# Another order of the matmuls inside a unit: how the walks over the eight rows turn, where the next unit goes on, and where z and b units begin

## Chip, core and metric

The kernel runs on one core of a Trainium2 chip. The metric is the device time of one execution in microseconds (us); the median of several runs counts. TensorE (PE, with its weight loads PEld), VectorE (DVE), ScalarE (ACT), GpSimd (POOL) and SyncE (SP, which here only issues DMAs) run beside each other.

## What is computed

One inference step of a hybrid decoder layer over 336 tokens: 16 meta and 256 prompt tokens, and 8 sequences of 8 new tokens. The parts that matter here, cut from the reference:

```python
h = rms_norm(x, norm_w)
proj = h @ w_in                     # 2048 -> 22592 columns
z, xbc, dt_raw, sc_b, sc_c, sc_h, sc_z, g_a, g_b = split_proj(proj)
xbc = silu(causal_dwconv(xbc, conv_prev, ssd_conv_w) + ssd_conv_b)
...                                 # Mamba-2 SSD over xs, B, C, dt -> y
y_a = gated_group_rms_norm(y, z, ssd_norm_w) @ w_ssd_out
u_c = causal_dwconv(sc_c * sc_h, sconv_prev, sconv_w)
y_b = (sc_b * u_c * silu(sc_z)) @ w_sconv_out
merged = sigmoid(g_a) * y_a + sigmoid(g_b) * y_b
out = x + merged @ w_o
```

All of it is float32. Almost all of the time is the matrix products, above all `h @ w_in`.

## The kernel before, in words

Activations lie with the channel on the partition: `hx` (L73) holds, for each of 16 row tiles k of 128 channels, the 336 tokens of `h`, once as a rounded high part (`hhi`) and once as the rest (`hlo`). One row tile is 336 floats, 1344 bytes of a partition. A **unit** (L128) makes 128 output columns for all tokens. It has two halves; each half takes 512 KB of weights (`wblk`, L96): a DMA to `wraw`, a copy on ACT to `whi`, a difference on DVE to `wlo`. These two hold eight blocks of 128 columns, 144 floats (576 bytes) apart, and the whole block is shifted by 16 floats (64 bytes) times `at` (L93).

A half then has 24 matmuls into one PSUM tile `pj` (`mm`, L123): for each of the eight rows k the three products hi·xh, hi·xl and lo·xh. So a unit has 48 matmuls, each with its own weight load. Which row comes when is set by the **plan** (`terms`, L116), and only by that; the sum is the same. `RISE` goes through rows 0 to 7 three times. `LAST` begins with row 7. `FALL2` goes down by two rows: 6 4 2 0 for hi·xh and hi·xl, then a turn by +7 to 7 5 3 1 for hi·xl, hi·xh and lo·xh, then a turn by +5 to 6 4 2 0 for lo·xh.

Units come one after another on PE, with two PSUM tiles in turn:

- Start: tiles 0 to 2 of the short convolution, partly before the norm is known (`uproj`, from `uhi` and `ulo`).
- Tiles j = 3 to 15 of the short convolution (L323), four units each: **c** (`FALL2`, 324 tokens, `at` 0) and **h** (`RISE`, 324 tokens, `at` = j mod 4) in `conv_in` (L236), then **z** and **b** (`RISE`, 320 tokens, `at` 0).
- 16 pairs of a gate unit and a unit of `w_sconv_out` (`LAST`), with the tables of the scan between them.
- Eight groups g of the scan. Each has six convolution units (`conv_tile`, L469): B and four x tiles with 336 tokens (`FALL2`, `at` 1), C with 324 tokens (`FALL2`, `at` 2), and four z units (`z_units`, L508, `RISE`, 320 tokens), with the scan's own steps, output units and some gates woven between them (L787).
- The rest: output units, gates, and the projection with `w_o`.

The queues of the other engines have the work of a unit in the order in which it is written. Nothing else orders the matmuls.

Of the kernel before, what the change touches and what calls it, by code (L numbers as in the profile page):

```python
# [9 lines left out]
AF = mybir.ActivationFunctionType  # L10
# [39 lines left out]
def tile_hybrid_step(ctx, tc, xT, w0, w1, w2, wdt, wso, wsc, wo, cmask, vec, hvec, convst, sconvst, xe_, fwe, h0T,  # L50
                     yA, yB, yE, convo, ssmp, ssms, sconvo):
    nc = tc.nc
# [37 lines left out]
    latest = {}  # L90
    AT_V, AT_Y, AT_O, AT_X, AT_C, AT_SC = 1, 3, 3, 1, 2, 0

# [20 lines left out]

    RISE, LAST, FALL2 = range(3)

    def terms(plan, hi, lo, xh, xl, nk):  # L116
        if plan == FALL2:
            even, odd = (list(range(i, nk, 2))[::-1] for i in range(2))
            return [(w, x, k) for w, x, q in ((hi, xh, even), (hi, xl, even), (hi, xl, odd), (hi, xh, odd), (lo, xh, odd),
                                              (lo, xh, even)) for k in q]  # L120
        return [(w, x, (k - (plan == LAST)) % nk) for w, x in ((hi, xh), (hi, xl), (lo, xh)) for k in range(nk)]

    def mm(out, hi, lo, xh, xl, base, nk, k0, first, last, plan=RISE):  # L123
        for i, (w, x, k) in enumerate(terms(plan, hi, lo, xh, xl, nk)):
# [3 lines left out]
    def unit(src, xh, xl, n, plan=RISE, at=0):  # L128
        pt = ps.tile([P, 512], F32, name="pj")
        for half in range(2):  # L130
            hi, lo = wblk(src[:, half * 1024:half * 1024 + 1024], at)
            mm(pt[:, :n], hi, lo, xh, xl, 0, 8, half * 8, half == 0, half == 1, plan)
        return pt[:, :n]

    def proj(src, t0, plan=RISE, at=0):
        return unit(src, lambda k: hhi[:, k, t0:T], lambda k: hlo[:, k, t0:T], T - t0, plan, at)
# [44 lines left out]
    with tc.tile_pool(name="pa", bufs=2) as pa:  # L181
# [50 lines left out]

        def uproj(src, t0, plan=RISE, at=0):
            return unit(src, lambda k: uhi[:, k, t0:T], lambda k: ulo[:, k, t0:T], T - t0, plan, at)

        def conv_in(j, pr, pre=None, fac=None, between=None):  # L236
            c_s = pa.tile([P, T - TC], F32, name="c_s")
            if fac is None:
                nc.scalar.activation(c_s, pre[0] if pre else pr(w2[16 + j], TC, FALL2, AT_SC), AF.Copy)
            else:  # L240
                nc.vector.tensor_tensor(c_s, pr(w2[16 + j], TC, FALL2, AT_SC), fac, mult)
            if between:
                between()
            ph = pre[1] if pre else pr(w2[32 + j], TC, at=j % 4)
            up = pa.tile([P, 338], F32, name=f"up{j}" if j < 2 else "up", bufs=1 if j < 2 else 2)
            ups = eights(up[:, 258:338], 10)
            nc.vector.tensor_tensor(up[:, :258], c_s[:, 2:260], ph[:, 2:260], mult)  # L247
            nc.vector.tensor_tensor(ups[:, :, 2:10], eights(c_s[:, 260:]), eights(ph[:, 260:]), mult)
            return up, ups
# [209 lines left out]
    with tc.tile_pool(name="pb", bufs=2) as pb:  # L459
# [588 lines left out]
```

## Time and profile before

| | |
|---|---|
| median of 3 runs | 1791.15 us (1789.12 to 1791.41) |
| the profiled execution | 1786.97 us |
| its span, first to last instruction | 1785.2 us |
| PE busy | 1776.8 us, 13006 matmuls |
| DVE, ACT, POOL busy | 1147.4, 829.1, 392.7 us |
| DMA | 331.33 MB, 186 GB/s over the span |
| granted clock of TensorE over the span | 0.999 |

The profiled execution took 1.8 us more than its span, and 4.2 us less than the median of the runs. A matmul is recorded for about 300 ns, but the next begins after some 140 ns; so its busy time says little, and the distance from start to start is the number to read. The timeline merges equal matmuls into one row: start, duration until the last of them ends, operands, and their count. The start of the next row less the start of this one, over the count, is the pace of PE.

### The profile page before, as it was taken

The numbers are of one execution on the slowest core, as the hardware profiler recorded it, in microseconds if no ns is written. First come the engines' busy times: TensorE is split into PE (matmuls) and PEld (weight loads), VectorE is DVE, ScalarE is ACT, GpSimd is POOL, SyncE is SP. The second block draws the span as 40 slices with busy tenths as digits, with TensorE's granted clock in tenths as the row PEclk, the third lists the DMA queues.
The fourth block names the chain that finished last, engine by engine and source line by source line (L and its number), as shares of the span: only waits on it lengthen the run. The fifth ranks groups of instructions, "written<-read, shape, count | busy, mean of one in ns | idle before, by whom it ended". The sixth has DMA issues, their size and how long they took to land.

```text
span 1785.2 us, 32410 instructions
## 1 busy us (share of the span) xinstructions
PE 1776.8 (100%) x13006; PEld 1760.2 (99%) x13006; DVE 1147.4 (64%) x1696; ACT 829.1 (46%) x1269; POOL 392.7 (22%) x398
## 2 busy tenths in 40 slices
PE   9999999999999999999999999999999999999998
PEld 9999999999999999999999999999999999999998
DVE  7845544454543335658587787877878778776644
ACT  6433333333333334646656354564546546443543
POOL 0100000000000001243262432534334253400012
PEclk9999999999999999999999999999999999999999
DMA  7444444444454557457567574665756657577553
GB/s 258 150 150 147 153 153 151 146 152 150 156 167 160 167 167 234 154 177 240 172 207 231 175 249 158 210 221 184 246 159 213 216 175 253 159 245 220 188 182 130
DMA packets 117286, 331.33 MB, mean 186 GB/s; under 512 B 20944, under 2 KB 37904, under 8 KB 117136
## 3 DMA queue, kind: packets, MB, share of 16 engines
q1 hardware_dynamic: 116272, 327.89, 56.2%
q8 instruction: 102, 1.67, 0.4%
q10 hardware_dynamic: 864, 1.38, 0.2%
q14 instruction: 48, 0.39, 0.1%
HBM read 296.34 MB, written 32.88 MB: 184 GB/s over the span
## 4 chain that ended last, share of the span: by engine, by line
PE 90%; DVE 4%; DMA 3%; ACT 2%; issue 1%; POOLq 0%; SPq 0%; POOL 0%; ACTq 0%; DVEq 0%
PE pj L125 83%; DMA wraw<-w 2%; PE yb L662 2%; DVE wlo L102 1%; DMA ssms<-h 1%; PE ms L648 1%; PE pj L230 1%; DVE h L728 1%; DVE cacc L483 1%; ACT whi L101 1%; PE yb L597 1%; ACT W L571 1%; PE pj L874 1%; PE ms L230 0%; PE ms L546 0%
## 5 line engine op out<-in xcount | busy, mean ns | idle before, releaser
L125 PE MATMUL pj<-hx,whi 128*128 128x320 f32 (+2 forms) x5760 | 899.9, 308 | 0.0
L125 PEld LDWEIGHTS pj<-hx,whi 128*128 128x128 f32 x5760 | 851.6, 188 | 4.6 <-ACT pad L474 1.7
L102 DVE TENSOR_TENSOR wlo<-wraw,whi 128x1024 fp32r<-128x1024 f32 x470 | 599.5, 1276 | 389.2 <-PE pj L125 193.2
L101 ACT ACTIVATE whi<-wraw 128x1024 fp32r<-128x1024 f32 x470 | 496.6, 1058 | 727.6 <-PE pj L125 592.0
L125 PE MATMUL pj<-hx,wlo 128*128 128x320 f32 (+2 forms) x2880 | 476.3, 307 | 0.0
L125 PEld LDWEIGHTS pj<-hx,wlo 128*128 128x128 f32 x2880 | 433.2, 188 | 0.0
L608 POOL TENSOR_TENSOR h<-h,decS 128x512 f32<-128x512 f32 x64 | 76.4, 1228 | 141.8 <-PE ms L648 141.8
L253 POOL COPY SCS<-up 128x2 f32<-128x2 f32 x16 | 20.9, 1307 | 353.1 <-DVE up L247 322.9
L125 PE MATMUL pj<-yh,whi 128*128 128x320 f32 x512 | 95.0, 307 | 1.5 <-ACT zs L515 0.8
L125 PE MATMUL pj<-yl,whi 128*128 128x320 f32 x512 | 93.5, 304 | 0.0
L125 PE MATMUL pj<-yh,wlo 128*128 128x320 f32 x512 | 93.4, 304 | 0.0
L483 DVE SCALAR_TENSOR_TENSOR cacc<-pad,V,cacc 128x360 f32<-128x360 f32 (+1 forms) x144 | 90.2, 626 | 2.0
L756 DVE TENSOR_TENSOR yan<-yan,pj 128x320 f32<-128x320 f32 x112 | 53.9, 484 | 54.4 <-PE pj L125 53.8
L476 POOL COPY pad<-cs 128x24 f32<-128x24 f32 x48 | 55.6, 1161 | 126.0 <-DVE cacc L483 113.0
L125 PEld LDWEIGHTS pj<-yh,whi 128*128 128x128 f32 x512 | 79.0, 188 | 4.1 <-DVE yan L756 1.6
L125 PEld LDWEIGHTS pj<-yl,whi 128*128 128x128 f32 x512 | 78.7, 188 | 0.0
L125 PEld LDWEIGHTS pj<-yh,wlo 128*128 128x128 f32 x512 | 78.5, 188 | 0.0
L477 POOL COPY cs<-pad 128x3 f32<-128x3 f32 x48 | 45.6, 950 | 77.1 <-ACT pad L474 76.6
L856 POOL TENSOR_TENSOR sacc<-sacc,sqf 128x320 f32<-128x320 f32 x13 | 15.5, 1194 | 187.4 <-DMA wraw<-wo 120.7
L580 POOL TENSOR_TENSOR xe<-xdt,tet 128x512 f32<-128x512 f32 (+1 forms) x24 | 30.4, 1266 | 99.4 <-DVE xdt L551 99.4
L486 ACT ACTIVATE cth<-cacc 128x360 f32<-128x360 f32 (+1 forms) x48 | 24.0, 499 | 42.7 <-DVE cacc L483 42.4
L125 PE MATMUL pj<-vhi,wlo 128*128 128x320 f32 x256 | 41.5, 304 | 0.0
(284 smaller groups left out, 1636.7 us busy)
## 6 DMA issues: line engine op xcount, KB each, us to landing
wraw<-w SPq DMA_DIRECT2D x346, 512.0 KB, 3.8
wraw<-wso SPq DMA_DIRECT2D x64, 512.0 KB, 3.6
wraw<-wsc SPq DMA_DIRECT2D x32, 512.0 KB, 3.8
h<-h0T SPq DMA_DIRECT2D x32, 512.0 KB, 5.0
ssms<-h SPq DMA_DIRECT2D x32, 512.0 KB, 4.6
wraw<-wo SPq DMA_DIRECT2D x32, 512.0 KB, 3.8
xq_d<-xe SPq DMA_DIRECT2D x16, 320.0 KB, 3.3
W<-ac_d SPq DMA_DIRECT2D x8, 576.0 KB, 5.9
```

Source lines behind the costliest of these rows:

```text
L101: latest["act"] = nc.scalar.activation(hi, raw, AF.Copy).ins
L102: latest["dve"] = nc.vector.tensor_tensor(lo, raw, fb(hi), sub).ins
L125: latest["pe"] = nc.tensor.matmul(out, w[:, base + k], x(k0 + k), start=first and i == 0, stop=last and i == 3 * nk - 1).ins
L253: nc.gpsimd.tensor_copy(SCS[:, j, 0, :], up[:, 256:258])
L476: nc.gpsimd.tensor_copy(smp[:, :, 0:3], cs[:, 1:9, :])
L477: nc.gpsimd.tensor_copy(cs[:, 0, :], pad[:, 272:275])
L483: nc.vector.scalar_tensor_tensor(acc[:, i0:], pad[:, i0 + k:360 + k], col(V_CW, 4 * j + k), acc[:, i0:], mult, add)
L486: nc.scalar.activation(th[:, i0:], acc[:, i0:], AF.Tanh)
L580: nc.gpsimd.tensor_tensor(split(xe[c][:n]), split(xdt[c][:n]), bc(hv(tet[:n, c, :], g), [n, 8, HP]), mult)
L608: nc.gpsimd.tensor_tensor(split(h0[b]), split(h0[b]), bc(hv(decS[:, b, :], g), [P, 8, HP]), mult)
L662: nc.tensor.matmul(yb[q * HP:(q + 1) * HP, t, t0:t0 + n], x[:, h * HP:(h + 1) * HP], w[:, h, :], start=i == 0, stop=i == 3)
L756: nc.vector.tensor_tensor(ya[:, m, :TV], ya[:, m, :TV], pp[:, :TV], add)
```

## The change

`terms` is written anew. A plan is now either a number, the row with which a rising walk begins, or a pair of a first row and four turns. The walk by two rows keeps its order of products; its two turns in each of the two halves are given by the plan. Where no first row is given, and in each second half, the walk goes on from the last row less two. So:

| unit | rows before, one half | rows now, first half, second half |
|---|---|---|
| c | 6420 6420 7531 7531 7531 6420, both halves | 6420 6420 7531 7531 7531 6420, 6420 6420 5317 5317 5317 4206 |
| h, j even | 01234567 three times, both halves | 4206 4206 3175 3175 3175 2064, 2064 2064 1753 1753 1753 0642 |
| h, j odd | 01234567 three times, `at` 1 or 3 | the same, `at` 0 |
| z and b, j even | 01234567 three times | from row j/2 mod 4 up |
| C of the scan | as c, `at` 2 | 6420 6420 5317 5317 5317 4206, 4206 4206 3175 3175 3175 2064, `at` 0 (g even) or 2 (g odd) |
| x, odd tiles | as c before | as C now, `at` 1 |
| B, and x of even tiles | as c before | the same |
| z of the scan, g = 1, 3, 5 | 01234567 three times | from row 1, 2, 3 up |

The 320-token units of the start take `at` 1 where they had 0. No instruction is added or taken away, and the other engines' work stands in the same order.

```diff
-    AT_V, AT_Y, AT_O, AT_X, AT_C, AT_SC = 1, 3, 3, 1, 2, 0
+    AT_V, AT_Y, AT_O, AT_X, AT_U = 1, 3, 3, 1, 1
...
-    def terms(plan, hi, lo, xh, xl, nk):
-        if plan == FALL2:
-            even, odd = (list(range(i, nk, 2))[::-1] for i in range(2))
-            return [(w, x, k) for w, x, q in ((hi, xh, even), (hi, xl, even), (hi, xl, odd), (hi, xh, odd), (lo, xh, odd),
-                                              (lo, xh, even)) for k in q]
-        return [(w, x, (k - (plan == LAST)) % nk) for w, x in ((hi, xh), (hi, xl), (lo, xh)) for k in range(nk)]
+    def terms(plan, half, hi, lo, xh, xl, nk):
+        if not isinstance(plan, tuple):
+            return [(w, x, (k + plan) % nk) for w, x in ((hi, xh), (hi, xl), (lo, xh)) for k in range(nk)]
+        first, turns = plan
+        k, out = first if half == 0 and first is not None else row[0] - 2, []
+        for i, (w, x) in enumerate(((hi, xh), (hi, xl), (hi, xl), (hi, xh), (lo, xh), (lo, xh))):
+            if i in (2, 5):
+                k += 2 + turns[2 * half + i // 5]
+            for _ in range(4):
+                out.append((w, x, k % nk))
+                k -= 2
+        row[0] = out[-1][2]
+        return out
...
-                nc.scalar.activation(c_s, pre[0] if pre else pr(w2[16 + j], TC, FALL2, AT_SC), AF.Copy)
+                nc.scalar.activation(c_s, pre[0] if pre else pr(w2[16 + j], TC, (6, (7, 5, 5, 5))), AF.Copy)
...
-            ph = pre[1] if pre else pr(w2[32 + j], TC, at=j % 4)
+            ph = pre[1] if pre else pr(w2[32 + j], TC, 0 if j % 2 else (None, (5, 5, 5, 5)))
...
-        bf = [raw_unit(uproj(w2[0], META), "bf")]
+        bf = [raw_unit(uproj(w2[0], META, 0, AT_U), "bf")]
...
-            nc.vector.tensor_tensor(f, uproj(w, META), rsb[:, META:], mult)
+            nc.vector.tensor_tensor(f, uproj(w, META, 0, AT_U), rsb[:, META:], mult)
...
+        def spin(j):
+            return 0 if j % 2 else j // 2 % 4
...
-            rest = [(j, *u, lambda: proj(w2[48 + j], META), lambda: proj(w2[j], META))]
+            rest = [(j, *u, lambda: proj(w2[48 + j], META, spin(j)), lambda: proj(w2[j], META, spin(j)))]
...
-            pp = proj(src, t0, FALL2, AT_C if t0 else AT_X)
+            if t0:
+                pp = proj(src, t0, (6, (5, 5, 5, 5)), 2 * (j % 2))
+            else:
+                pp = proj(src, t0, (6, (5, 5, 5, 5) if j % 2 and j < 32 else (7, 5, 7, 5)), AT_X)
...
-                pz = proj(w1[4 * g + t], META)
+                pz = proj(w1[4 * g + t], META, g // 2 + 1 if g in (1, 3, 5) else 0)
```

The order of instructions names tiles and not rows of a tile. Since `hx` holds both parts of `h`, it shows the change at one place alone: PE, the h unit of tile 2, which still reads `uhi` and `ulo`. Before:

```order
L125 MATMUL pj<-uhi,whi 128x324 x8
L125 MATMUL pj<-ulo,whi 128x324 x8
L125 MATMUL pj<-uhi,wlo 128x324 x8
L125 MATMUL pj<-uhi,whi 128x324 x8
L125 MATMUL pj<-ulo,whi 128x324 x8
L125 MATMUL pj<-uhi,wlo 128x324 x8
L125 MATMUL pj<-hx,whi 128x320 x16
```

The same place on PE now:

```order
L132 MATMUL pj<-uhi,whi 128x324 x4
L132 MATMUL pj<-ulo,whi 128x324 x8
L132 MATMUL pj<-uhi,whi 128x324 x4
L132 MATMUL pj<-uhi,wlo 128x324 x8
L132 MATMUL pj<-uhi,whi 128x324 x4
L132 MATMUL pj<-ulo,whi 128x324 x8
L132 MATMUL pj<-uhi,whi 128x324 x4
L132 MATMUL pj<-uhi,wlo 128x324 x8
L132 MATMUL pj<-hx,whi 128x320 x16
```

The three runs of eight have become the walk by two: four rows with the high part, eight with the low, four with the high again. At the c, h and z units of tile 4 the rows on PE read as before, since only the row k inside `hx` and `whi` differs; with the PSUM and weight tiles' numbers, c and h there now:

```order
L132 MATMUL pj_1334<-hx_80,whi_1337 128x324 x16
L132 MATMUL pj_1334<-hx_80,wlo_1338 128x324 x8
...
L132 MATMUL pj_1396<-hx_80,whi_1399 128x324 x16
L132 MATMUL pj_1396<-hx_80,wlo_1400 128x324 x8
...
L132 MATMUL pj_1467<-hx_80,whi_1470 128x320 x16
```

Sixteen matmuls with the high weights and eight with the low in each half, as before; nothing is moved past another engine's work.

## Rows read from the trace of the kernel before

**Rows 1.** The page: busy time of engines, granted clock in 40 slices.

```profile
PE 1776.8 (100%) x13006; PEld 1760.2 (99%) x13006; DVE 1147.4 (64%) x1696; ACT 829.1 (46%) x1269; POOL 392.7 (22%) x398
...
PEclk9999999999999999999999999999999999999999
```

**Rows 2.** PE's timeline (start us, us, group): tiles 3, 4, and 5's c.

```profile
91.53 2.50 PE L125 MATMUL pj<-hx,whi 128*128 128x324 f32 x16
...
98.55 2.53 PE L125 MATMUL pj<-hx,whi 128*128 128x324 f32 x16
...
105.67 2.48 PE L125 MATMUL pj<-hx,whi 128*128 128x320 f32 x16
...
112.63 2.48 PE L125 MATMUL pj<-hx,whi 128*128 128x320 f32 x16
...
119.59 2.55 PE L125 MATMUL pj<-hx,whi 128*128 128x324 f32 x16
...
126.78 2.53 PE L125 MATMUL pj<-hx,whi 128*128 128x324 f32 x16
...
133.89 2.45 PE L125 MATMUL pj<-hx,whi 128*128 128x320 f32 x16
...
140.71 2.43 PE L125 MATMUL pj<-hx,whi 128*128 128x320 f32 x16
...
147.51 2.50 PE L125 MATMUL pj<-hx,whi 128*128 128x324 f32 x16
...
154.53 2.54 PE L125 MATMUL pj<-hx,whi 128*128 128x324 f32 x16
```

**Rows 3.** The same view inside the c unit of tile 5, by narrow windows.

```profile
148.71 1.31 PE L125 MATMUL pj<-hx,whi 128*128 128x324 f32 x8
...
149.85 1.31 PE L125 MATMUL pj<-hx,wlo 128*128 128x324 f32 x8
...
151.00 2.51 PE L125 MATMUL pj<-hx,whi 128*128 128x324 f32 x16
...
152.15 1.35 PE L125 MATMUL pj<-hx,whi 128*128 128x324 f32 x8
...
153.35 1.35 PE L125 MATMUL pj<-hx,wlo 128*128 128x324 f32 x8
```

**Rows 4.** The same view: the gate unit after tile 15, and what follows it.

```profile
455.13 2.48 PE L125 MATMUL pj<-hx,whi 128*128 128x320 f32 x16
...
462.09 1.32 PE L125 MATMUL pj<-vhi,whi 128*128 128x320 f32 x8
```

**Rows 5.** The same view: two 320-token units of the start, one after the other.

```profile
49.67 1.34 PE L125 MATMUL pj<-uhi,whi 128*128 128x320 f32 x8
...
56.72 1.33 PE L125 MATMUL pj<-uhi,whi 128*128 128x320 f32 x8
```

**Rows 6.** The same view, group 0 of the scan: C, two x tiles.

```profile
689.22 2.48 PE L125 MATMUL pj<-hx,whi 128*128 128x324 f32 x16
691.54 1.33 PE L125 MATMUL pj<-hx,wlo 128*128 128x324 f32 x8
692.72 2.50 PE L125 MATMUL pj<-hx,whi 128*128 128x324 f32 x16
...
696.23 2.58 PE L125 MATMUL pj<-hx,whi 128*128 128x336 f32 x16
...
703.45 2.57 PE L125 MATMUL pj<-hx,whi 128*128 128x336 f32 x16
```

**Rows 7.** The same view: z units of the scan, groups 1 and 2.

```profile
837.12 2.43 PE L125 MATMUL pj<-hx,whi 128*128 128x320 f32 x16
...
840.52 2.43 PE L125 MATMUL pj<-hx,whi 128*128 128x320 f32 x16
...
945.89 2.48 PE L125 MATMUL pj<-hx,whi 128*128 128x320 f32 x16
...
949.37 2.48 PE L125 MATMUL pj<-hx,whi 128*128 128x320 f32 x16
```

More of the change, by code (lines that the diff above doesn't have):

```diff
@@ L112, in behind, with mm, unit @@
                                                                          mybir.DependencyReason.DATA), reason="step")
-    RISE, LAST, FALL2 = range(3)
-    def terms(plan, hi, lo, xh, xl, nk):
-        if plan == FALL2:
-            even, odd = (list(range(i, nk, 2))[::-1] for i in range(2))
-            return [(w, x, k) for w, x, q in ((hi, xh, even), (hi, xl, even), (hi, xl, odd), (hi, xh, odd), (lo, xh, odd),
-                                              (lo, xh, even)) for k in q]
-        return [(w, x, (k - (plan == LAST)) % nk) for w, x in ((hi, xh), (hi, xl), (lo, xh)) for k in range(nk)]
-    def mm(out, hi, lo, xh, xl, base, nk, k0, first, last, plan=RISE):
-        for i, (w, x, k) in enumerate(terms(plan, hi, lo, xh, xl, nk)):
+    row = [0]
+    def terms(plan, half, hi, lo, xh, xl, nk):
[11 more added lines that the diff above has]
+        return out
+    def mm(out, hi, lo, xh, xl, base, nk, k0, first, last, plan=0, half=0):
+        for i, (w, x, k) in enumerate(terms(plan, half, hi, lo, xh, xl, nk)):
             latest["pe"] = nc.tensor.matmul(out, w[:, base + k], x(k0 + k), start=first and i == 0,
                                             stop=last and i == 3 * nk - 1).ins
-    def unit(src, xh, xl, n, plan=RISE, at=0):
+    def unit(src, xh, xl, n, plan=0, at=0):
         pt = ps.tile([P, 512], F32, name="pj")
@@ L131, in unit, with proj @@
             hi, lo = wblk(src[:, half * 1024:half * 1024 + 1024], at)
-            mm(pt[:, :n], hi, lo, xh, xl, 0, 8, half * 8, half == 0, half == 1, plan)
+            mm(pt[:, :n], hi, lo, xh, xl, 0, 8, half * 8, half == 0, half == 1, plan, half)
         return pt[:, :n]
-    def proj(src, t0, plan=RISE, at=0):
+    def proj(src, t0, plan=0, at=0):
         return unit(src, lambda k: hhi[:, k, t0:T], lambda k: hlo[:, k, t0:T], T - t0, plan, at)
@@ L231, in tile_hybrid_step, with uproj @@
                                      start=k == 0 and j == 0, stop=k == 15 and j == 2)
-        def uproj(src, t0, plan=RISE, at=0):
+        def uproj(src, t0, plan=0, at=0):
             return unit(src, lambda k: uhi[:, k, t0:T], lambda k: ulo[:, k, t0:T], T - t0, plan, at)
@@ L238, in conv_in @@
             if fac is None:
-                nc.scalar.activation(c_s, pre[0] if pre else pr(w2[16 + j], TC, FALL2, AT_SC), AF.Copy)
+                nc.scalar.activation(c_s, pre[0] if pre else pr(w2[16 + j], TC, (6, (7, 5, 5, 5))), AF.Copy)
             else:
-                nc.vector.tensor_tensor(c_s, pr(w2[16 + j], TC, FALL2, AT_SC), fac, mult)
+                nc.vector.tensor_tensor(c_s, pr(w2[16 + j], TC, (6, (7, 5, 5, 5))), fac, mult)
             if between:
                 between()
-            ph = pre[1] if pre else pr(w2[32 + j], TC, at=j % 4)
+            ph = pre[1] if pre else pr(w2[32 + j], TC, 0 if j % 2 else (None, (5, 5, 5, 5)))
             up = pa.tile([P, 338], F32, name=f"up{j}" if j < 2 else "up", bufs=1 if j < 2 else 2)
@@ L448, in tile_hybrid_step @@
             nc.scalar.activation(th, pg, AF.Tanh, scale=0.5)
-            py = unit(wsc[m], lambda k: vhi[:, k, :], lambda k: vlo[:, k, :], TV, LAST, AT_V)
+            py = unit(wsc[m], lambda k: vhi[:, k, :], lambda k: vlo[:, k, :], TV, 7, AT_V)
             nc.vector.scalar_tensor_tensor(th, th, 1.0, py, add, mult)
```

## Prediction

> **What bounds the kernel now.** [...] DVE at 1147.4 us and the others have slack. So the number of matmuls and the pace of each sets the time. The change leaves the number alone; what it can move is the pace, and that is read in the timeline from start to start.
>
> There the reader sees that equal units don't take equal time. Tile 3's z and b take 112.63 − 105.67 = 6.96 us and again 6.96; tile 4's, with the same 48 matmuls of the same shape and no wait, take 6.82 and 6.80 [rows 2]. That is 0.142 against 0.145 us for one. The c of tile 4 takes 126.78 − 119.59 = 7.19 us, those of tiles 3 and 5 take 7.02 [rows 2]. An h takes 7.12 and 7.11 [rows 2].
>
> Inside tile 5's c [rows 2, 3]: eight matmuls from 147.51 to 148.71 take 1.20; the next eight, after the turn by +7, take 1.14, or 0.143 each; the eight with the low weights, a turn by +5 among them, take 1.15; the next eight again 1.15; then, after the second turn by +7, eight take 1.20, and the last eight lead to the h at 154.53, 1.18 later. So at 324 tokens there is a **quick pace** of 0.143, 6.88 us a unit, and a slow one of 0.148 to 0.150, 7.12 to 7.2. PE keeps one of the two for many matmuls, and a turn can throw it from one into the other: the first +7 helped, the second hurt, the +5 did neither. An h, which steps by one row, is always slow [rows 2].
>
> My reading, from the code and these rows: what counts is where the block of weights being loaded lies against the row being streamed. Rows are 1344 bytes apart and blocks 576, and both leave 64 when divided by 256; so a step of +5 is like a step of +1, and −2 like +2. That a bank of memory stands behind it no row shows.
>
> **The change, part by part.** The sum is made on the profiled execution, 1786.97 us, of which the 52 units of tiles 3 to 15 take 455.13 − 91.53 = 363.60 us [rows 2, 4]. At the quick pace they would take 26 × 6.88 + 26 × 6.80 = 355.68. So 7.92 us is all there is to win in this part.
>
> *c, 13 units.* Only the first +7 is kept. I expect 1.20 for the first eight and the quick pace after it, with three turns by +5. One costs 0 to 0.01 us: the eight with one took 1.15 where 8 × 0.143 is 1.14 to 1.15 [rows 3]. At 0.01 a unit takes 6.88 + 0.05 + 0.03 = 6.96. Tiles 3, 4 and 5 average 7.08 [rows 2], but the slow kind came at 3 of the 13, so the mean is 7.06. Gain 13 × 0.10 = 1.3 us.
>
> *h of even tiles, 6 units.* They go on with the walk of c by −2, the step that runs quick inside c. Four turns at 0.01: 6.92 instead of 7.12. Gain 6 × 0.20 = 1.2 us. h of odd tiles: still a rising walk, and the h at `at` 0 (tile 4, 7.11) and the one at 3 (tile 3, 7.12) are alike [rows 2]: 0.
>
> *z and b.* Read in the same way, 7 of the 13 tiles (3, 6, 7, 10, 11, 14, 15) have the slow kind, near 6.96, and 6 the quick one; which it is goes with the tile modulo 4, and so with the `at` of the h ahead. (The kinds add up: 10 × 7.02 + 3 × 7.19 + 13 × 7.115 + 14 × 6.96 + 12 × 6.81 is 363.4, and the 52 units take 363.60 [rows 2, 4].) Now h of odd tiles is as that of tile 4, behind which z was quick [rows 2], and even tiles come from a quick h and begin at another row. If all are quick, with 0.02 for entering, the 26 take 26 × 6.82; now they take 26 × 6.80 and 2.4 more. Gain 1.9 us. If PE comes in quick, the gate unit of 455.13 and the unit after it are quick as well: the first takes 6.96 now [rows 4], so 2 × 0.16 = 0.3.
>
> *The start.* Three units of 320 tokens get `at` 1; one takes 56.72 − 49.67 = 7.05 [rows 5], and 6.80 is the least. No row shows that shift on these tiles. Bounds: no gain, and 3 × 0.25 = 0.75; I take the middle, 0.35. Tile 2's h, now a walk, and tiles 1 and 2's c: 0 to 0.3, taken as 0.1.
>
> *Group of the scan.* An x unit takes (703.45 − 696.23) = 7.22 [rows 6], or 0.150 each, and the two turns by +7 stand in that. For 16 odd x tiles they become +5: 0 to 0.03 us each by how little 7.22 leaves over 48 × 0.150, so 0 to 0.5 in all, taken as 0.25. C takes 696.23 − 689.22 = 7.01 [rows 6]. For even g it gets c's shift and +5 turns: 6.95, gain 4 × 0.06 = 0.25. For odd g the shift of 2 stays, and there the eight with a turn by +5 take 1.18 [rows 6], 0.03 over; four such turns give back what the +7 turns cost. I take 0, between −0.2 and 0.2.
>
> *z of the scan.* Group 1's takes 840.52 − 837.12 = 3.40 for a half, group 2's 3.48 [rows 7]. In groups 2, 4 and 6 three of four units are slow: 9 × 0.16 = 1.4 us. How PE comes out of the scan's steps decides, and the change meets this with other starting rows and another C ahead. Bounds: −1 (odd groups become slow instead) to 1.4; I take half, 0.7.
>
> Nothing is added beside it: DVE, ACT, the queues and the DMAs have the same work in the same order, and PE meets a half's low weights at its 17th matmul as before. PE would need them 0.1 us a unit sooner; with DVE idle for a third of the span, that is covered.
>
> The sum: 1.3 + 1.2 + 1.9 + 0.3 + 0.45 + 0.5 + 0.7 = **6.4 us**. The profiled execution would take 1780.6; set against the median of the runs, 4.2 above it, 1784.8.
>
> **The rivals.**
>
> *The pace at entry stays a toss-up.* c and h gain their 2.5, the start and the scan's convolutions 0.9, but half of z and b units stay slow, as now. Then 3.4 us: 1787.8. For it: the z of tile 3 and of tile 4 follow h units of the same pace and differ [rows 2], so the entry hangs on something finer than the rows tell. Against it: it went with the tile modulo 4 without an exception.
>
> *The order of rows doesn't matter by itself*, and the two paces come from elsewhere, so that the new order finds the same mixture: 1791.2. For it is only that I infer the cause. Against it: in tile 5's c the pace changed at the turns [rows 3]. [...]
>
> *The turn by +5 throws PE into the slow pace and keeps it there*, as the second +7 did at 152.15 [rows 3]. Its places are the turns from even to odd rows in the second half of c and in all of the walking h, C and odd x units. Then c would be like tile 4's, 7.19, and so would h of even tiles; z and b behind them would all be slow, and C too. Price: c 13 × (7.19 − 7.06) = 1.7, h 6 × 0.07 = 0.4, z and b 26 × 0.16 − 2.4 = 1.7, C 8 × 0.17 = 1.3: **+5.1 us, 1796.3**. It decides if one turn by +5 costs more than the 0.01 of the low eight. Against it: the one +5 at that shift in tile 5 left PE quick for another twelve matmuls [rows 3]. For it: that one leads from odd to even, and three of the new ones lead from even to odd, which no row shows.
>
> **How the numbers follow.** The forecast gets 0.62, the toss-up 0.20, the order that doesn't matter 0.06, the slow turn 0.12. For the range I take the forecast's unknowns at their better ends: 0.6 more from the start, 0.45 from the scan's convolutions, 0.7 from its z units, and 0.9 where entries and turns cost nothing; 9.05 us in all give 1782.1, and 0.3 is left for the scatter of the runs. The other way it reaches past the toss-up to 1790.5, most of the way to no effect, since the two cases beyond hold 0.18. Left out are most of the slow turn and of the case of no effect. What can be told from no change is about 0.2%, 3.6 us. Faster by more: the forecast but for its worst end, 0.60, and near half of the toss-up, 0.10, so 0.70. Within it: the rest of these two and the third, 0.19. Slower: 0.11.
>
> **What would show it.** Right: in tile 5 after the change the c takes about 6.96 with one stretch of eight at 1.20 at its beginning, and all z and b rows lie 6.80 to 6.84 apart; the h of tile 4 takes 6.92; the gate unit behind tile 15 takes 6.80. Wrong: an h of an even tile at 7.1 or more, or low eights of c at 1.19 (the slow turn); z rows 6.96 apart behind either kind of h (the toss-up). A PE group with idle time ahead of it that it doesn't have now would mean that a wait, and not the pace, took the gain.

## The result, and the profile after

The changed kernel takes 1785.01 us (median of 9 runs, 1783.32 to 1786.1), beside 1789.46 us for the kernel before in 9 runs of the same chip (1787.65 to 1791.83). The ratio is 0.9974, with a 95% interval of 0.9964 to 0.9983: 4.45 us won, 3.0 to 6.4 by the interval. The profiled execution took 1784.7 us and its span is 1782.9. The spans of the two profiles lie only 2.3 us apart; the execution of before that was profiled was one of its quickest, 2.5 us under that median of 9. What lies behind the 2.3 us is taken up below.

The page of the changed kernel has for PE, where [rows 1] has 1776.8:

```profile
PE 1773.6 (99%) x13006; PEld 1756.8 (99%) x13006; DVE 1147.0 (64%) x1696; ACT 829.5 (47%) x1269; POOL 390.4 (22%) x398
```

PE's timeline of the changed kernel (start, duration, group), tiles 3, 4 and 5, answers to [rows 2] and [rows 3]. Helper lines moved, so that L125 is now L132:

```profile
91.46 2.55 PE L132 MATMUL pj<-hx,whi 128*128 128x324 f32 x16
...
98.65 2.54 PE L132 MATMUL pj<-hx,whi 128*128 128x324 f32 x16
...
105.78 2.45 PE L132 MATMUL pj<-hx,whi 128*128 128x320 f32 x16
...
112.60 2.43 PE L132 MATMUL pj<-hx,whi 128*128 128x320 f32 x16
...
119.40 2.50 PE L132 MATMUL pj<-hx,whi 128*128 128x324 f32 x16
...
126.34 2.46 PE L132 MATMUL pj<-hx,whi 128*128 128x324 f32 x16
...
133.24 2.44 PE L132 MATMUL pj<-hx,whi 128*128 128x320 f32 x16
...
140.05 2.43 PE L132 MATMUL pj<-hx,whi 128*128 128x320 f32 x16
...
146.85 2.50 PE L132 MATMUL pj<-hx,whi 128*128 128x324 f32 x16
149.18 1.31 PE L132 MATMUL pj<-hx,wlo 128*128 128x324 f32 x8
150.34 2.46 PE L132 MATMUL pj<-hx,whi 128*128 128x324 f32 x16
...
153.78 2.54 PE L132 MATMUL pj<-hx,whi 128*128 128x324 f32 x16
```

From start to start: tile 3's z takes 112.60 − 105.78 = 6.82 and its b 6.80, where [rows 2] has 6.96 twice. The h of tile 4, now a walk, takes 133.24 − 126.34 = 6.90 instead of 7.11. Tile 5's c takes 6.93 instead of 7.02, and its last 24 matmuls 153.78 − 150.34 = 3.44, which is 24 × 0.143: with all turns but the first by +5 the quick pace holds to the end. But tile 3's c takes 98.65 − 91.46 = 7.19 instead of 7.02, and so do those of tiles 7, 11 and 15.

The same view at the places of [rows 4 to 7]: the start, the gate behind tile 15, group 0's C and x, and z of groups 1 and 2:

```profile
49.65 1.33 PE L132 MATMUL pj<-uhi,whi 128*128 128x320 f32 x8
...
56.69 1.34 PE L132 MATMUL pj<-uhi,whi 128*128 128x320 f32 x8
...
451.10 2.43 PE L132 MATMUL pj<-hx,whi 128*128 128x320 f32 x16
...
457.90 1.30 PE L132 MATMUL pj<-vhi,whi 128*128 128x320 f32 x8
...
684.90 2.56 PE L132 MATMUL pj<-hx,whi 128*128 128x324 f32 x16
...
692.10 2.58 PE L132 MATMUL pj<-hx,whi 128*128 128x336 f32 x16
...
699.32 2.56 PE L132 MATMUL pj<-hx,whi 128*128 128x336 f32 x16
...
836.37 2.43 PE L132 MATMUL pj<-hx,whi 128*128 128x320 f32 x16
839.77 2.43 PE L132 MATMUL pj<-hx,whi 128*128 128x320 f32 x16
...
945.75 2.48 PE L132 MATMUL pj<-hx,whi 128*128 128x320 f32 x16
949.23 2.48 PE L132 MATMUL pj<-hx,whi 128*128 128x320 f32 x16
```

The start's unit still takes 7.04; the gate takes 6.80 instead of 6.96; C takes 7.20 instead of 7.01, a loss; half a z takes 3.40 in group 1 and 3.48 in group 2, as before. PE reaches group 0's C 689.22 − 684.90 = 4.3 us earlier than before, and only 2.3 us of that are left at the end of this span. Part of the loss is the scan's own units, part is two waits, which the timeline shows in brackets (idle us, and who ended it), the first behind z of group 5, the second behind z of group 7. `zs` is the copy of a z unit that ACT takes out of its PSUM tile:

```profile
1297.72 0.86 PE L132 MATMUL pj<-yh,whi 128*128 128x320 f32 x4 [0.53 <-ACT zs L528]
...
1518.56 0.84 PE L132 MATMUL pj<-yh,whi 128*128 128x320 f32 x4 [1.19 <-ACT zs L528]
```

Of these two the profile of before has the second alone, and shorter:

```profile
1520.88 0.86 PE L125 MATMUL pj<-yh,whi 128*128 128x320 f32 x4 [0.79 <-ACT zs L515]
```

### The profile page after: what moved, and what is told of

Same layout as the page of the kernel before. It is cut to its first block, busy times and chain, and to the rows that moved or that the text cites. A ratio compares the mean times of both kernels' runs of the same rounds, so it can differ in the third digit from the quotient of the medians.

```text
span 1782.9 us, 32410 instructions
## 1 busy us (share of the span) xinstructions
PE 1773.6 (99%) x13006; PEld 1756.8 (99%) x13006; DVE 1147.0 (64%) x1696; ACT 829.5 (47%) x1269; POOL 390.4 (22%) x398
## 4 chain that ended last, share of the span: by engine, by line
PE 90%; DVE 4%; DMA 3%; ACT 2%; issue 1%; POOLq 0%; SPq 0%; POOL 0%; ACTq 0%; DVEq 0%
PE pj L132 83%; DMA wraw<-w 2%; PE yb L675 2%; DVE wlo L102 1%; DMA ssms<-h 1%; PE ms L661 1%; PE pj L237 1%; DVE h L741 1%; DVE cacc L496 1%; ACT whi L101 1%; PE yb L610 1%; ACT W L584 1%; PE pj L887 1%; PE ms L237 0%; PE ms L559 0%
## 5 line engine op out<-in xcount | busy, mean ns | idle before, releaser
L132 PE MATMUL pj<-hx,whi 128*128 128x320 f32 (+2 forms) x5760 | 897.9, 308 | 0.0
L132 PEld LDWEIGHTS pj<-hx,whi 128*128 128x128 f32 x5760 | 849.8, 188 | 4.6 <-ACT pad L487 1.7
L132 PE MATMUL pj<-hx,wlo 128*128 128x320 f32 (+2 forms) x2880 | 475.3, 307 | 0.0
L132 PEld LDWEIGHTS pj<-hx,wlo 128*128 128x128 f32 x2880 | 432.2, 188 | 0.0
L132 PE MATMUL pj<-yh,whi 128*128 128x320 f32 x512 | 95.3, 308 | 2.2 <-ACT zs L528 1.7
L132 PE MATMUL pj<-yl,whi 128*128 128x320 f32 x512 | 93.6, 304 | 0.0
L132 PE MATMUL pj<-yh,wlo 128*128 128x320 f32 x512 | 93.4, 304 | 0.0
L132 PEld LDWEIGHTS pj<-yh,whi 128*128 128x128 f32 x512 | 79.0, 188 | 5.1 <-ACT zs L528 2.2
L132 PEld LDWEIGHTS pj<-yl,whi 128*128 128x128 f32 x512 | 78.7, 188 | 0.0
L132 PEld LDWEIGHTS pj<-yh,wlo 128*128 128x128 f32 x512 | 78.5, 188 | 0.0
L132 PE MATMUL pj<-vlo,whi 128*128 128x320 f32 x256 | 41.5, 304 | 0.0
```

## Experiments

"Over the quick pace" means a unit's time from its start to the next one's, less 6.80 us for 320 tokens, 6.88 for 324 and 7.12 for 336. The first two are 48 matmuls at 0.1417 and 0.1433 us, steady steps of the trace; 7.12 is a mark to count from and no pace that was seen, since the quickest steady step at 336 tokens is 0.150 us, 7.19 a unit. A lead of PE is its lead over the profile of before, counted from the start of its first whole unit, which lies at 27.4 to 27.9 us in the profiles; so counted, the changed kernel's is 4.4 us at the scan and 2.3 at the end. All ratios are to runs of the kernel before on the same chip. e5 to e8 were run once each, so that their times say nothing and only their rows are read. Lines of code are cut to the part that changes.

### e10: what made z and b quick

The kernel before, with h's shift taken out (written in the changed kernel's `terms`, so that its helper is L132 too):

```diff
-            ph = pre[1] if pre else pr(w2[32 + j], TC, at=j % 4)
+            ph = pre[1] if pre else pr(w2[32 + j], TC)
```

> The kernel before with one thing altered: the weights of h lie at shift 0 in every tile instead of 0 to 3 by the tile's number modulo 4; no order of rows changes. It tells what made all z and b quick in the changed kernel. Theory 'the shift of the h ahead': z and b of all 13 tiles take 6.80 to 6.84 us here, 2.2 us of the changed kernel's gain, h stays at 7.11 and c as before; time 1.8 to 2.4 us below the kernel before (ratio 0.9987 to 0.999). Rival 'the new first rows of z, or the walk of h': z and b of tiles 3, 6, 7, 10, 11, 14 and 15 stay at 6.96, and the time is that of the kernel before within 0.5 us. Rival 'toss-up': about half slow, but in other tiles.

Ratio 0.9981 (0.9973 to 0.9990). Its timeline at tile 3 and the start of tile 4:

```profile
91.51 2.50 PE L132 MATMUL pj<-hx,whi 128*128 128x324 f32 x16
...
98.53 2.54 PE L132 MATMUL pj<-hx,whi 128*128 128x324 f32 x16
...
105.65 2.45 PE L132 MATMUL pj<-hx,whi 128*128 128x320 f32 x16
...
112.48 2.43 PE L132 MATMUL pj<-hx,whi 128*128 128x320 f32 x16
```

Tile 3's z now takes 112.48 − 105.65 = 6.83. In all 13 tiles z takes 6.825 and b 6.80, though no row's order has changed. Over the quick pace z and b together have 0.32 us instead of 2.46, and c 1.87 instead of 2.34, because the slow c of tiles 4, 8 and 12 went as well, where c as before had been expected; h stays at 7.12. PE comes to the scan with a lead of 2.9 us, of which 1.4 are left at the end of this span. So the shift of h decided for z and b, and dropping it alone, without any walk, wins two thirds of the 4.4 us that the changed kernel wins ahead of the scan.

### e4 and e12: what made four c units slow

e4 turns the first rows of z and b on by one:

```diff
-            return 0 if j % 2 else j // 2 % 4
+            return 0 if j % 2 else (j // 2 + 1) % 4
```

> The changed kernel with the first rows of the even tiles' z and b turned on by one: tile 2 begins at row 2, tile 4 at 3, 6 at 0, 8 at 1, 10 at 2, 12 at 3, 14 at 0. In the changed kernel c is slow (7.20 us) in tiles 3, 7, 11 and 15, and quick (6.94) in all others. Theory 'the row on which the unit ahead ends decides': an end on an even row (first row 1 or 3) makes the next c slow, so the slow c are now those of tiles 5, 9 and 13, and tiles 3, 7, 11 and 15 take 6.94; 0.26 us less in all. Rival 'it goes with the tile's number modulo 4', say by the buffer that the weights fall in: c of 3, 7, 11 and 15 stay at 7.20 and those of 5, 9 and 13 at 6.94. z and b stay between 6.80 and 6.84 under both.

Ratio 0.9981 (0.9972 to 0.9991). The slow c have moved: tile 5's is

```profile
146.95 2.56 PE L132 MATMUL pj<-hx,whi 128*128 128x324 f32 x16
...
154.15 1.06 PE L132 MATMUL pj<-hx,whi 128*128 128x324 f32 x6
```

154.15 − 146.95 = 7.20, as are those of tiles 9 and 13, and all others take 6.94. So the c that were entered behind a unit that ended on an even row were slow, 7.20 against 6.94, and their first turn by +7 didn't mend that: in the changed kernel's trace, groups of four matmuls behind that turn take 593, 597 and 605 ns in tile 3, where in tile 4 they take 573, 573 and 579.

e12 undoes the first rows altogether:

```diff
-            return 0 if j % 2 else j // 2 % 4
+            return 0
```

> The changed kernel with one part undone: z and b of even tiles start at row 0, as in the kernel before. Theory 'the first rows did harm and no good': z and b stay quick (what made them so is the shift of h), and c of tiles 3, 7, 11 and 15 takes 6.94 us instead of 7.20, so that PE comes to the scan 1.0 us earlier than in the changed kernel, 5.4 us ahead of the kernel before. Rival 'the first rows keep z and b quick behind a walking h': z or b of even tiles fall back to 6.96, up to 12 x 0.16 = 1.9 us lost against 1.0 won.

Ratio 0.9981 (0.9973 to 0.9990). All 13 c take 6.94, tile 3's among them:

```profile
91.49 2.50 PE L132 MATMUL pj<-hx,whi 128*128 128x324 f32 x16
...
98.43 0.76 PE L132 MATMUL pj<-hx,whi 128*128 128x324 f32 x4
```

z takes 6.83 to 6.84 and b 6.80, so the first rows weren't needed for them. PE comes to the scan with a lead of 5.2 us, 0.85 more than the changed kernel: c wins 1.03, z gives back 0.16, tile 2's counted in. The timed ratio can't tell 0.9 us.

### e6: which turns keep the pace

Every c entered behind row 1, every h a walk, with turns of one kind by tile:

```diff
-            ph = pre[1] if pre else pr(w2[32 + j], TC, 0 if j % 2 else (None, (5, 5, 5, 5)))
+            ph = pre[1] if pre else pr(w2[32 + j], TC, (None, (2 * (j % 4) + 1,) * 4))
...
-            return 0 if j % 2 else j // 2 % 4
+            return 2
```

> The changed kernel with two edits in tiles 2 to 15: z and b of every tile start at row 2, so that each c is entered behind row 1, and every h walks on where c ended, with its four turns all by +1, +3, +5 or +7, by the tile's number modulo 4 (0: +1, 1: +3, 2: +5, 3: +7). Theory of the prediction 'turns count modulo 4 (256 bytes)': +1 is like +5, 6 ns a turn and the quick pace kept, so h of tiles 4, 6, 8, 10, 12 and 14 takes 6.90 us; +3 and +7 are alike, the sort that ended the quick pace in the kernel before, so h of tiles 3, 5, 7, 9, 11, 13 and 15 takes 7.05 to 7.20. Rival 'any turn between even and odd rows costs one slow step and nothing more': 6.90 for all. Rival 'each turn is its own case': 6.90 for +5 alone. All c should be quick, 6.94, behind an h that ended quick.

The h and then the z of tiles 4 (turns by +1), 5 (+3) and 7 (+7):

```profile
126.25 2.46 PE L132 MATMUL pj<-hx,whi 128*128 128x324 f32 x16
...
133.15 1.02 PE L132 MATMUL pj<-hx,whi 128*128 128x320 f32 x6
...
153.69 2.51 PE L132 MATMUL pj<-hx,whi 128*128 128x324 f32 x16
...
160.75 0.46 PE L132 MATMUL pj<-hx,whi 128*128 128x320 f32 x2
...
208.78 2.51 PE L132 MATMUL pj<-hx,whi 128*128 128x324 f32 x16
...
215.84 1.34 PE L132 MATMUL pj<-hx,whi 128*128 128x320 f32 x8
```

6.90 for +1, 7.06 for +3 and for +7; +5, in tiles 6, 10 and 14, gives 6.90. Each kind is the same in each of its tiles to 2 ns. So +1 is like +5 and +3 like +7, as the reading of 256 bytes has it; four rows are 5376 bytes, 21 times 256. The rivals fall. Inside the h of tile 5 the trace shows what the turns by +3 do: groups of four matmuls take 573 and 578 ns, 595 to 601 from the first turn to the third, 573 to 577 behind that, and 598 behind the fourth. So one kind of turn both begins and ends the slow pace.

### e7: the place of the weights

The same walks, with c's weights shifted by 64 bytes times a number by tile, and h a walk by +5 everywhere (the edit of h is the first of e9's):

```diff
-pr(w2[16 + j], TC, (6, (7, 5, 5, 5)))
+pr(w2[16 + j], TC, (6, (7, 5, 5, 5)), (0, 1, 2, 3, 4, 6, 8)[(j - 3) % 7] if j > 2 else 0)
...
-            return 0 if j % 2 else j // 2 % 4
+            return 2
```

> The changed kernel with z and b of every tile starting at row 2, every h walking on where c ended with turns by +5 (7.12 us in odd tiles now, 6.90 expected), and c's weights shifted in memory by 0, 64, 128, 192, 256, 384 and 512 bytes from tile to tile (tile 3: 0, 4: 64, 5: 128, 6: 192, 7: 256, 8: 384, 9: 512, 10: 0 and so on); the walk of c is the same in all. Theory of the prediction 'where the weight block lies against the row counts, modulo 256 bytes': c at 256 and 512 takes 6.94 as at 0, c at 384 is as at 128, and 64, 128 and 192 differ from 0, 7.0 us or more. Rival 'only the order of rows counts': 6.94 at every shift. Rival 'a longer period': 256 or 384 differ from 0 or 128, and 512 is as 0.

The c and then the h of tiles 3 (shift 0), 5 (128 bytes) and 7 (256 bytes):

```profile
91.44 2.50 PE L132 MATMUL pj<-hx,whi 128*128 128x324 f32 x16
...
98.37 0.88 PE L132 MATMUL pj<-hx,whi 128*128 128x324 f32 x5
...
146.78 2.50 PE L132 MATMUL pj<-hx,whi 128*128 128x324 f32 x16
...
153.82 1.37 PE L132 MATMUL pj<-hx,whi 128*128 128x324 f32 x8
...
202.57 2.50 PE L132 MATMUL pj<-hx,whi 128*128 128x324 f32 x16
...
209.51 0.74 PE L132 MATMUL pj<-hx,whi 128*128 128x324 f32 x4
```

| shift, bytes | 0 | 64 | 128 | 192 | 256 | 384 | 512 |
|---|---|---|---|---|---|---|---|
| c, us | 6.94 | 7.10 | 7.04 | 7.11 | 6.94 | 7.04 | 6.94 |
| h behind it, us | 6.90 | 7.19 | 7.21 | 7.21 | 6.90 | 7.21 | 6.90 |

256 and 512 are as 0, and 384 is as 128: the place counts modulo 256 bytes. The walking h behind a slow c takes 7.19 to 7.21 us, more than any rising h of tiles 3 to 15 in the profiles of before and after (7.12 to 7.13), and behind a quick c 6.90: the turns by +5 kept the pace that they met.

### e3: the slow C of even groups

```diff
-                pp = proj(src, t0, (6, (5, 5, 5, 5)), 2 * (j % 2))
+                pp = proj(src, t0, (6, (5, 5, 5, 5) if j % 2 else (7, 5, 5, 5)), 2 * (j % 2))
```

> The changed kernel with one number altered: C of even groups makes its first turn by +7 instead of +5. Theory 'a first turn by +7 ends the slow pace with which a unit is entered, a +5 keeps it': C of groups 0, 2, 4 and 6 takes 6.95 us instead of 7.20, 1.0 us in all, as c of tiles 4 and 5 do (the first eight matmuls there run as C's first eight do). Rival 'the +7 helps only behind some entries' (in the changed kernel it did not help c of tiles 3, 7, 11 and 15): C stays at 7.15 to 7.20. The total is then 1.0 us lower or unchanged, which the runs can hardly tell; the rows of C decide.

Ratio 0.9977 (0.9968 to 0.9986). C of group 0, and then the first x:

```profile
684.93 2.50 PE L132 MATMUL pj<-hx,whi 128*128 128x324 f32 x16
...
691.88 0.32 PE L132 MATMUL pj<-hx,whi 128*128 128x336 f32 x1
```

6.95, and 6.95 in groups 2, 4 and 6, where the changed kernel has 7.20. The first +7 was what the plan for C lacked. Beside e4 this shows the limit: +7 mended this entry, and not that of a c behind an even row (7.20). (The B ahead of C ends on an even row too, row 0, but its weights lie at another shift.)

### e1 and e2: the two halves of the change apart

e1 keeps c, h, z and b of the tiles, and has the scan and the start as before; e2 the reverse, but for the start, which is as before too. Their edits on the changed kernel, e1's first:

```diff
-    AT_V, AT_Y, AT_O, AT_X, AT_U = 1, 3, 3, 1, 1
+    AT_V, AT_Y, AT_O, AT_X, AT_U = 1, 3, 3, 1, 0
...
-                pp = proj(src, t0, (6, (5, 5, 5, 5)), 2 * (j % 2))
+                pp = proj(src, t0, (6, (7, 5, 7, 5)), 2)
...
-                pp = proj(src, t0, (6, (5, 5, 5, 5) if j % 2 and j < 32 else (7, 5, 7, 5)), AT_X)
+                pp = proj(src, t0, (6, (7, 5, 7, 5)), AT_X)
...
-                pz = proj(w1[4 * g + t], META, g // 2 + 1 if g in (1, 3, 5) else 0)
+                pz = proj(w1[4 * g + t], META)
```

```diff
-    AT_V, AT_Y, AT_O, AT_X, AT_U = 1, 3, 3, 1, 1
+    AT_V, AT_Y, AT_O, AT_X, AT_U = 1, 3, 3, 1, 0
...
-(6, (7, 5, 5, 5))
+(6, (7, 5, 7, 5))
...
-            ph = pre[1] if pre else pr(w2[32 + j], TC, 0 if j % 2 else (None, (5, 5, 5, 5)))
+            ph = pre[1] if pre else pr(w2[32 + j], TC, 0, j % 4)
...
-            return 0 if j % 2 else j // 2 % 4
+            return 0
```

> Only the part of the change on tiles 2 to 15 (c, h, z, b); the first units and the whole scan walk their rows as in the kernel before. Theory 'the scan's own new order gives it back': in the changed kernel PE is 4.37 us ahead of the kernel before at the scan's first convolution and 2.3 us at the end, because C of even groups takes 7.20 us instead of 7.01 and some x and z units got slower. Then here PE comes to the scan some 4.3 us ahead and is still 4 us or more ahead at the end, C of group 0 takes 7.01 again, and the time is 4.0 to 4.8 us below the kernel before (ratio 0.9973 to 0.9978). Rival 'waits give it back': whatever the order in the scan, PE runs into work of ACT that it used to find done (the wait of 0.53 us at 1297.72 in the changed kernel); then the lead shrinks to 2 to 3 us here too, with a PE wait for zs at an output unit.

> Only the part of the change on the scan (C, odd x tiles, the z units' first row); the first units and tiles 2 to 15 walk as before. Theory 'the scan's own order costs': C of even groups starts slow and has no turn by +7 that could end it, so it takes 7.20 us instead of 7.01 (four times 0.19 = 0.7 us), x about 0.1 in all and z 0.2 to 0.3; the time is 0.5 to 1.3 us above the kernel before (ratio 1.0003 to 1.0007). Rival 'C is slow in the changed kernel only because PE enters the scan from other units': then C of group 0 takes 7.0 us or less here and the scan costs nothing or wins up to 0.7 us.

e1: ratio 0.9976 (0.9967 to 0.9985); e2: 1.0002 (0.9993 to 1.0011). The tiles carry the gain; the scan's part wins nothing that the runs can tell. By the rows, in e2 C takes 7.20 in even groups as in the changed kernel, and C, x and z lose 0.71, 0.14 and 0.53 us, 0.27 of the last being a wait behind the last z of group 7; in e1 they keep what they had before, but for 0.05 us. So the scan's loss belongs to its own order. But e1's second expectation, a lead kept to the end, failed: of 4.20 us at the scan's start 0.80 were left at the end of its span, with PE waiting 3.3 us for zs at the two places named above, where the kernel before waits 0.8. Another 0.57 us went in four output units behind the scan: from 1581.76 on they run at 145 ns a matmul, 6.96 us a unit, where both kernels take 6.80 there with the same walk and the same places; e3 and e10 show the same. They part after a short stop in the middle of the first of these units, so the pace at an entry doesn't hang on order and place alone. Waits are a part of the story, and e8 says which.

### e8: the changed kernel once more

> The changed kernel once more, with nothing altered: a second profile of it. Theory 'the pace of units is fixed by the order, and what is lost in the scan is waits that differ from one execution to the next': every unit's pace repeats to a few ns (c of tile 3 at 7.20, h of tile 4 at 6.90, C of group 0 at 7.20), while the waits of PE for ACT's zs at the ends of groups 4 and 7 (0.53 us and 1.49 us of gap in the first profile) come out otherwise, by half a us or more. Rival 'the waits belong to the change': they repeat to 0.1 us.

Unit by unit the two profiles agree to a few ns where PE doesn't wait: C 7.20, tile 3's c 7.20, tile 4's h 6.90; c over the quick pace sums to 1820 and 1821 ns, z of the scan to 4545 and 4548. The waits don't agree. Behind z of group 5 there is none now, and behind z of group 7 it is 1.86 us instead of 1.19 (and not 1.49, as the expectation has it):

```profile
1518.18 0.90 PE L132 MATMUL pj<-yh,whi 128*128 128x320 f32 x4 [1.86 <-ACT zs L528]
```

What decides at the first place is ACT ahead of it. These are the rows of its copy of a weight block, of the first profile and then of the second:

```profile
1288.03 1.06 ACT L101 ACTIVATE whi<-wraw 128x1024 fp32r<-128x1024 f32 x1 [5.35 <-DMA wraw<-w]
```

```profile
1286.96 1.06 ACT L101 ACTIVATE whi<-wraw 128x1024 fp32r<-128x1024 f32 x1 [3.87 <-DMA wraw<-w]
```

ACT stood idle 5.35 us for a transfer in one and 3.87 in the other; from there it works without a gap to the zs for which PE waits, 1.0 us later in the first. PE waits 0.53 us in the one and not in the other. So the wait behind group 5 hangs on when a weight transfer lands, and the waits differ from execution to execution of one program: PE's lead at the end is 2.32 us in one profile and 1.23 in the other.

### e5: first rows of z in the scan

```diff
-                pz = proj(w1[4 * g + t], META, g // 2 + 1 if g in (1, 3, 5) else 0)
+                pz = proj(w1[4 * g + t], META, g)
```

> The changed kernel with z units of scan group g starting at row g, a table of all eight first rows (in the changed kernel groups 1, 3 and 5 start at rows 1, 2 and 3, all others at 0). Theory 'the entry of each z unit falls quick or slow by its first row, given what came ahead': the sum over quick pace of a group's four units, 0.82 us in groups 2, 4 and 6 and 0.36 to 0.54 in the others now, changes with the row and one or two rows bring all four units to the quick 6.80, so that a better table could win up to 1.2 us over the scan. Rival 'the small steps between z units set the pace at entry, whatever the first row': even groups stay at 0.8 and odd ones near 0.4 for every row. The total moves by less than 1.5 us under both; the rows of z decide.

Four units of a group over the quick pace, in us, with the time that PE takes to come in from the small steps between them:

| group = first row | 0 | 1 | 2 | 3 | 4 | 5 | 6 | 7 |
|---|---|---|---|---|---|---|---|---|
| sum | 0.24 | 0.54 | 0.51 | 0.36 | 0.83 | 0.67 | 0.51 | 0.36 |

A wait of 0.79 us behind the last unit of group 7 is left out. Rows 2 and 6 are alike unit by unit, and so are 3 and 7: modulo 4 again. Row 4 in group 4 is as row 0 there was. Rows 1 and 5 are alike in three units and differ in the third, 6.93 and 7.06; there the group seems to count, since in e11, with row 1 in all odd groups, that unit takes 6.92 in group 1 and 7.06 in groups 3, 5 and 7. The row does change the pace at entry, against the rival; but no one row is right for all four units, and what is left with row 3, some 0.1 a unit, is the coming in and not the pace.

### e9 and e11: put together

e9, on the changed kernel (the edits that make the first units walk without a shift aren't shown):

```diff
-            ph = pre[1] if pre else pr(w2[32 + j], TC, 0 if j % 2 else (None, (5, 5, 5, 5)))
+            ph = pre[1] if pre else pr(w2[32 + j], TC, (None, (5, 5, 5, 5)))
...
-            return 0 if j % 2 else j // 2 % 4
+            return 2
...
-                pp = proj(src, t0, (6, (5, 5, 5, 5)), 2 * (j % 2))
+                pp = proj(src, t0, (6, (7, 5, 5, 5)))
...
-                pp = proj(src, t0, (6, (5, 5, 5, 5) if j % 2 and j < 32 else (7, 5, 7, 5)), AT_X)
+                pp = proj(src, t0, (6, (7 if j % 4 == 1 and 3 < j < 32 else 5, 5, 5, 5)), AT_X)
...
-                pz = proj(w1[4 * g + t], META, g // 2 + 1 if g in (1, 3, 5) else 0)
+                pz = proj(w1[4 * g + t], META, (0, 3, 3, 3, 1, 3, 2, 3)[g])
```

> What the rows so far say, put together on top of the changed kernel: z and b of every tile start at row 2; every h walks on from c with turns by +5; C of every group has no shift and the turns +7, +5, +5, +5; B and x have only turns by +5, but for a first +7 in the second x of groups 1 to 7, which is entered slow; z of the scan starts at rows 0, 3, 3, 3, 1, 3, 2, 3 by group; the first bf, zf1 and bf1 units walk by two rows with no shift. Theory 'each pace is set by the walk and the entry, and adds up': against the changed kernel c wins 1.1 us, h of odd tiles 7 x 0.22 = 1.5, C 1.2, x and B 0.8 to 0.9, z of the scan 0.5 to 1.5, the first units 0 to 0.6; 5 to 6.5 us together, a time near 1779 to 1780 us and a ratio to the kernel before of 0.994 to 0.9955. Rival 'waits take it': ACT's and the DMAs' work in the scan is the same, PE arrives earlier and waits; then PE's lead over the kernel before at the scan's first convolution is 7 us or more, but less than 5 us of it is left at the end, and the ratio stays above 0.9965.

1781.24 us, ratio 0.9956 (0.9942 to 0.9969). Every h takes 6.90 and every c 6.94; C 6.95; PE comes to the scan 7.2 us ahead and ends its span 7.9 ahead, so the rival falls. But the time is above the 1779 to 1780 expected. The step that failed is z of the scan: row 3 made the first two slow in groups 1, 2, 3, 5 and 7 (group 1's first took 833.64 − 826.55 = 7.09), a loss of 0.33 us where 0.5 to 1.5 were to be won. In e5 row 3 had left both of them quick in group 3 behind an x that took the same 7.28, so that the first row doesn't fix this entry by itself; what else does stays open. B and x won 0.15 us where 0.8 to 0.9 were expected, because the third x of a group became slow (7.40 instead of 7.33), and the walk in the first units won nothing.

e11, on e9, with the start's edits taken back:

```diff
-                pp = proj(src, t0, (6, (7 if j % 4 == 1 and 3 < j < 32 else 5, 5, 5, 5)), AT_X)
+                pp = proj(src, t0, (6, (7 if j % 4 in (1, 2) and 3 < j < 32 else 5, 5, 5, 5)), AT_X)
...
-                pz = proj(w1[4 * g + t], META, (0, 3, 3, 3, 1, 3, 2, 3)[g])
+                pz = proj(w1[4 * g + t], META, (0 if g == 0 else (2, 2, 1, 3)[t] if g % 2 else (1, 1, 1, 3)[t]))
```

> The kernel of e9 with what its trace showed put in: the first bf, zf1 and bf1 as in the changed kernel (the walk made them 0.02 us slower each), the third x of groups 1 to 7 gets a first turn by +7 as the second has (in e9 it was entered slow and stayed so, 0.281 us over the quick pace instead of 0.212), and each z unit of the scan gets a first row of its own: 1, 1, 1, 3 for even groups, 2, 2, 1, 3 for odd ones (in e9 row 3 made the first two z of five groups slow, rows 1 and 2 did not). Theory 'each entry has its row': z of groups 1 to 7 takes 0.35 to 0.55 us over the quick pace a group instead of 0.5 to 0.84, x 0.08 less a group; 1.5 to 2.5 us less than e9 in the profile, a time of 1779 to 1780 us, ratio 0.9943 to 0.995. Rival 'rows don't carry over from one kernel to the next': the z units fall slow elsewhere and the time stays at 1781 us.

1780.09 us, ratio 0.9957 (0.9944 to 0.9971): beside 1788.65 us for the kernel before in runs next to it. It is below both kernels, though its interval still touches that of the changed kernel; by the ratio it and e9 are the same. z of the scan is 1.59 us nearer to the quick pace than in e9, x 0.24 nearer (0.03 a group, where 0.08 was expected). But the lead at the end is that of e9, 7.9 us: PE waits 1.8 us for zs behind group 7, where in e9 it waits 1.2, and makes shorter stops at the ends of groups 1, 3 and 5. So these rows did carry over, and the time did not follow. PE's line of its page:

```profile
PE 1767.9 (99%) x13006; PEld 1750.9 (99%) x13006; DVE 1143.6 (64%) x1696; ACT 829.8 (47%) x1269; POOL 391.3 (22%) x398
```

## Why the prediction was right, and where its steps were not

The direction, the place and the time came out as forecast: 1784.8 said, 1785.01 measured. But the time rests on the median of 1791.15 of the three runs shown; later groups of runs of the kernel before gave 1788.65 to 1789.46. That the two agree to 0.2 us is luck: a base 1.7 us too high and a gain 2 us too large cancelled. The gain is the fairer measure: 6.4 us forecast, 4.45 timed, and 3.3 by the rows.

Term by term, from start to start in the two timelines:

| term | forecast gain, us | measured |
|---|---|---|
| c, 13 units | 1.3 | 0.52 |
| h of even tiles | 1.2 | 1.3 |
| z and b, 26 units | 1.9 | 2.15 |
| gate and the unit behind it | 0.3 | 0.3 |
| start, with tiles 1 and 2's c and h | 0.45 | 0.1 |
| C | 0.25 | −0.71 |
| x | 0.25 | −0.14 |
| z of the scan | 0.7 | −0.25 |
| sum | 6.4 | 3.3 |

*h, and the price of a +5 turn*: right. A turn by +5 costs 6 ns, from even to odd rows as from odd to even (in tile 4's h four matmuls take 573 ns without one and 579 with one), and the slow-turn rival falls with the first h that took 6.90. e6 shows that the reading behind it was right too.

*z and b*: the size was right, the reason half so. The prediction said that which kind it is goes with h's shift, and for even tiles it also leaned on the quick h and the new first row. e10 shows that the shift alone does it (6.825 and 6.80 us), e12 that the first row wasn't needed. The toss-up rival falls for these units; in the scan the entry of z does hang on something finer than row and place (e9 beside e5).

*c*: the mechanism was right and the entry was missed. Nine units did as forecast, 6.94. The step that failed is "I expect 1.20 for the first eight and the quick pace after it", which took the entry of tile 5 for that of all. The new first rows 1 and 3 made z and b end on an even row, and four c paid 0.26 us each (e4, e12). Against e10, where c has its old turns and takes 7.02 everywhere, the turns' gain of 9 × 0.083 and this loss of 4 × 0.175 cancel; nearly all of the 0.52 that c won is e10's too (0.46), and so comes from the shift of h.

*C*: the same mistake. The prediction counted "c's shift and +5 turns" at 6.95 and didn't carry over that c's plan starts with +7 and C's with +5. C is entered slow, and with turns by +5 alone it stayed so: 7.20, beside 6.95 with a first +7 (e3).

*x*: the turn's price was right, 0.02 us a unit where x is entered quick (group 0's second x took 7.21 and now takes 7.19). In the second x of groups 1 to 7, which is entered slow, the +7 had been what ended that, and without it the slow stretch lasts longer: 7.28 instead of 7.24, 0.04 lost each.

*z of the scan*: half of a bound was taken without a row. Even groups kept row 0 and their 0.83 us; groups 1 and 3, with new first rows, got a slow unit each. The prediction's lower bound of −1, "odd groups become slow instead", had the sign and the place.

*The start*: the shift by 64 bytes changed nothing (7.05 before, 7.04 now).

*"The order of rows doesn't matter by itself"* falls with e3 and e6, where nothing but turns differs: C takes 7.20 or 6.95, and h 6.90 or 7.06. e7 adds that the place matters with the order kept: one walk, the same 48 matmuls, no wait, and 6.94 or 7.11 us by where the weights lie. What in the chip makes the difference no run shows.

*From the sum to the time*: the rows give 4.4 us ahead of the scan less 1.1 in it, 3.3, just inside the timed interval of 3.0 to 6.4. The profiles' spans show 2.3, since the two executions differ in waits (e8). The prediction's "nothing is added beside it" was too short: the transfers are the same, but PE arrives earlier, and at two places behind z units it then stands for ACT, which itself stood for weights that hadn't landed. How much of the lead this takes on average, one profile of a kernel can't say, and the timed runs scatter too much; that stays open.

## What to carry to other kernels

Where one engine is always busy with equal instructions, compare equal units from start to start: two paces of one unit, here 6.96 and 6.80 us for a z, are a gain to be had without any instruction less. Change the layout of one operand first and by itself (here the shift of h, worth 2.9 us ahead of the scan), since a change of order and a change of place can each win or spoil what the other brings (the new first rows made four c 0.26 us slower each, e12). A unit's pace can depend on how it is entered, as c's did, 6.94 or 7.20 us with one walk (e4), so that a plan tried in one unit is worth what its entry makes of it in the next; and of a lead that is won early, look for the place where a transfer takes it back.

## What the runs showed of the hardware

- The pace of TensorE, at a granted clock of 0.999 and with no wait, depended in c on where the weight block lies against the streamed rows, modulo 256 bytes: it took 6.94, 7.10, 7.04 and 7.11 us at shifts of 0, 64, 128 and 192 bytes, and 6.94, 7.04 and 6.94 at 256, 384 and 512 (e7).
- The same walk had more than one steady pace, 143.3 and about 150 ns a matmul at 324 tokens (c of tiles 4 and 3 in the changed kernel, 6.94 and 7.20 us). In h units without a shift, turns by +1 and +5 rows left it at the quick one for 6 ns each, 6.90 us a unit; turns by +3 switched it in both directions, from 573 to 595 ns for four matmuls and back, 7.06 us a unit, as with turns by +7 (e6). In C a first turn by +7 gave 6.95 us, one by +5 7.20 (e3).
- The times of units were reproduced to a few ns from one execution of a program to the next (the 13 c over the quick pace 1820 and 1821 ns together), while the waits for weight transfers were not: ACT stood 5.35 and 3.87 us for the same transfer (e8). Behind a stop, units of the same order and place came in at either pace: output units behind the scan took 6.80 us in both kernels and 6.96 in e1, e3 and e10.
